# Shared scatter banks for the last two expert pairs, another order of value products, and three smaller edits, in an encoder layer

## The chip, the cores and the metric

The kernel runs on one core of a Trainium2 chip. The metric is the device time of one execution in microseconds (us). The core has a matmul engine (TensorE, PE in the profile; PEld is its weight load), a vector engine (VectorE, DVE), a scalar engine (ScalarE, ACT), GpSimd (POOL) and SyncE (SP), which here issues the DMA transfers. PE adds up products in PSUM, which has eight banks of 512 fp32 values per partition; the other engines read the sums from there.

## The reference

One layer of an encoder on 512 tokens of 1024 channels, with a final norm, all in fp32:

```python
h = rms_norm(x);  u = h @ w_in
c = silu(layer_norm(depthwise_conv31(glu(u[:, :512]))))      # 256 channels
a = dilated_attention(rotary(q), rotary(k), v)               # 12 heads of 64, 3 branches
x = x + concat(rms_norm(c), rms_norm(a)) @ w_out
x = x + cross_attention(rms_norm(x), rms_norm(mem))          # 4 heads of 256, 256 memory tokens
h = rms_norm(x)                                              # expert layer from here
group = top1(softmax(h @ w_group + b_group))                 # 4 groups
two experts = top2 of the group's 8 by h @ w_router + b_router
for each expert e: y_e = (silu(h @ w1[e]) * (h @ w3[e])) @ w2[e]   # 512 hidden columns
x = x + gate1 * y_e1 + gate2 * y_e2
out = rms_norm(x)
```

## The kernel before

**Tokens and precision.** The 512 tokens are four tiles of 128 (`NT = 4`). Where operands are rounded to the fp32r format, a value is split into a high part and the remainder, and the products run with both; `split` (line 109) lets ACT copy the high half and DVE (or the engine given as `eng`) subtract it from the value (line 115).

**Attention.** The 12 heads run in six pairs. `head_softmax` makes, for each of a head's four query tiles, the scores (lines 560 and 561), a masked maximum, the exponential (ACT, line 569) and the reciprocal of the sum, and GpSimd multiplies the row with it (line 572, tile `pw`). `head_transposed` turns each `pw` on PE (line 582) and collects the result in `pt`, two query tiles per `pt`. `attend_out` then makes the value products of a pair (line 596): two halves of the queries (256 columns each), four key tiles, two heads; head 0 writes partitions 0 to 63 of the PSUM tile `o` and head 1 partitions 64 to 127. This part is written in program order, and a list scheduler with priorities places the instructions of each engine: at each step the engine takes, of what is ready by its model, the piece of highest priority. GpSimd also has the convolution's taps (lines 423, 424, 434, 435) and the last step of the rotary embedding (lines 504 and 505). PE's rows of line 147 that stand between these are products of the input projection for the following pairs.

**Route.** `route_tile` computes for each token tile the group, the two experts and the gates on small DVE operations (lines 901 to 954), the matrix `M` of chosen experts (line 925), and from that, by a product on PE, the rank `RK` of each token within its expert. It also fills `hm`, the normalised tokens in high and low halves that the gather products read. For the last tile (t = 3) ACT writes the scaled row `hn` first, and the low halves are made by GpSimd.

**Experts.** Each expert has 64 slots. The 32 experts run in 16 pairs. `hot` builds a one-hot matrix from `RK`; `take` gathers by products `hm` x one-hot; `put` stores the result as `xT`. Weights stream through a ring of regions in SBUF (`ring`, 512 KB per DMA, SP line 1014), issued in order as regions come free. `experts_up` and `experts_down` compute the hidden and the output rows with fp32 products of 64 columns; the scatter adds an expert pair's rows back to the tokens by a product with a one-hot matrix (`ct`) in PSUM, and DVE adds the PSUM bank to the residual `xacc` (line 1231). This part is written in the order in which it runs.

**The end.** `experts_last` handles the last pair, n + 3. Its output columns come in three groups: out(0) has columns 0 to 511, out(1) 512 to 767 and out(2) 768 to 1023. `between` scatters the pair before it, n + 2, with banks of its own. Then the norm: ACT (line 1332) or DVE (line 1343) sums squares of each tile and column group into `fss`; `finish_out` adds them up for all four tiles, GpSimd raises them to the power -0.5, and ACT and DVE scale the tiles, each of which SP then writes out.

Of the kernel before, what the change touches and what calls it, by code (L numbers as in the profile page):

```python
# [8 lines left out]
F32 = mybir.dt.float32  # L9
# [3 lines left out]
AF = mybir.ActivationFunctionType  # L13
# [71 lines left out]
class K:  # L85
# [502 lines left out]
    def attend_out(self, j, pts, v):  # L588

        nc = self.nc  # L590
        o = self.ps("o")
        vo = (j % 2) * 128
        for half in range(2):
            for kt in range(NT):
                for i in range(2):
                    nc.tensor.matmul(o[i * 64:i * 64 + 64, half * 256:half * 256 + 256],
                                     v[kt][:, vo + i * 64:vo + i * 64 + 64], pts[i][half][:, kt, :],
                                     start=kt == 0, stop=kt == NT - 1)
        self.split(o, self.aT[0][:, 2 + j, :], self.aT[1][:, 2 + j, :], scale=self.VT[:, V_AO + j:V_AO + j + 1])
        return o  # L600
# [284 lines left out]
    def route_tile(self, t, p, ss, rs, lgs):  # L885
# [35 lines left out]
        key2, k2 = keys(em, m2, NE, "b")  # L921
        oh2 = row("oh2", NE)
        V.tensor_scalar(oh2, key2, k2, None, op0=ALU.is_equal)
        M = self.M[:, t, :]
        V.scalar_tensor_tensor(M, no1, 0.0, oh2, op0=ALU.is_lt, op1=ALU.add)
        with self.tc.high_priority(offset=-60 if t < NT - 1 else 0):

            h = self.xacc[:, t, :]
            for b in range(2):
                c = slice(b * 512, b * 512 + 512)  # L930
                parts = lambda v: v.rearrange("q (b m) -> q b m", b=2)
                hi, lo = parts(self.hm[t][:, 0, c]), parts(self.hm[t][:, 1, c])
                turned = h[:, c].rearrange("q (m b) -> q b m", b=2)
                if t < NT - 1:
                    self.split(turned, hi, lo, scale=r)
                else:
                    hn = self.rh.tile([128, 512], F32, name="hn", tag="hmT")
                    nc.scalar.activation(parts(hn[:]), turned, AF.Copy, scale=r)
                    self.split(hn, self.hm[t][:, 0, c], self.hm[t][:, 1, c], eng=nc.gpsimd)

            gx, gs = row("gx", NG), one("gs")
            ngm = one("ngm")
            V.tensor_scalar(ngm, gm, -1.0, None, op0=ALU.mult)
            nc.scalar.activation(gx, gl, AF.Exp, bias=ngm, scale=1.0, accum_out=gs)
            e2 = one("e2")
            V.tensor_tensor(e2, m2, m1, op=ALU.subtract)
            nc.scalar.activation(e2, e2, AF.Exp)
            g1 = one("g1")
            V.scalar_tensor_tensor(g1, e2, 1.0, gs, op0=ALU.add, op1=ALU.mult)
            V.reciprocal(g1, g1)  # L950
            V.tensor_tensor(e2, e2, g1, op=ALU.mult)
            G = self.G[:, t, :]
            V.tensor_scalar(G, no1, 0.0, g1, op0=ALU.is_lt, op1=ALU.mult)
            V.scalar_tensor_tensor(G, oh2, e2, G, op0=ALU.mult, op1=ALU.add)
# [78 lines left out]

    def hot(self, oh, d, t):

        self.nc.vector.tensor_tensor(oh[:, t, :].rearrange("p (e s) -> p e s", s=CAP),
                                     self.iota[:].unsqueeze(1).to_broadcast([128, 4, CAP]),
                                     self.RK[:, t, 4 * d:4 * d + 4].unsqueeze(2).to_broadcast([128, 4, CAP]), op=ALU.is_equal)

# [18 lines left out]
    def first_gather(self):  # L1058


        oh, xT = self.slots()
        ps = [self.ps(tag) for tag in ("tr", "s", "s", "tr")]

        def add(t, chunks=range(DC)):
            if chunks[0] == 0:
                self.hot(oh, 0, t)
            for cc in chunks:
                self.take(ps[cc // 2], oh, cc, t, t == 0 and cc % 2 == 0, t == NT - 1 and cc % 2 == 1)

        def end():  # L1070
            x = xT()
            put = lambda chunks: [self.put(x, ps[cc // 2], cc) for cc in chunks]

            def rest():
                add(NT - 1, range(DC // 2, DC))
                put(range(DC // 2, DC))

            put(range(DC // 2))
            return oh, x, rest
        return add, end  # L1080
# [152 lines left out]
    def experts(self, gathered):  # L1233
# [8 lines left out]
        with self.in_order():  # L1242
            gt = None
            for d in range(NE // 4 - 1):
# [21 lines left out]
                if d:  # L1266
# [16 lines left out]
            ys, ct = None, c2  # L1283
            self.hidden_turned((n + 3,))
            ys = self.experts_down(n + 2, now[:, 0:1])
        self.experts_last(n + 3, self.hidden(n + 3), ct[:, 1, :], now[:, 1:2],
                          lambda: self.scatter_pair(ct[:, 0, :], ys, end))

    def experts_last(self, pr, hT, ct, gt, between):

        self.finish_begin()
        y2 = [self.wsp.tile([128, 2, 512], F32R, name="y2", tag="whi") for _ in range(2)]
# [2 lines left out]
        def out(j, before=None):  # L1295
            c0, c1 = groups[j]
            w = ((lambda e, k: self.piece(pr, 2, k, None)[:, e, :]) if j == 0 else
                 (lambda e, k: self.last_piece(j - 1, k)[:, e, :]))
            ys = self.outputs(w, hT, gt, c1 - c0, y2[j % 2], before)
            return [(ct, ys)], c0, c1 - c0, ("o", "m", "tr", "tr")  # L1300

        with self.in_order():
            first = out(0)
            between()
            self.scatter(*first)
            todo = out(1)
        self.finish_part(0, 0, 512, range(NT))
        with self.queued():
            last = out(2, lambda: self.scatter_tile(0, *todo))
            for t in range(1, NT):  # L1310
                self.scatter_tile(t, *todo)
            self.finish_part(1, 512, 768, range(NT))
            self.scatter(*last, lambda t: self.finish_last(t))
            self.finish_out()

    def finish_begin(self):

# [18 lines left out]

    def finish_last(self, t):

        if t < NT // 2:
            self.finish_part(2, 768, D, [t])  # L1340
        else:
            x = self.xacc[:, t, 768:D]
            self.nc.vector.tensor_tensor_reduce(self.fk[:, 0:256], x, x, 1.0 / D, 0.0, ALU.mult, ALU.add,
                                                self.fss[:, t, 2:3])

    def finish_out(self):

        nc = self.nc
        r = self.frs
        nc.vector.tensor_reduce(r, self.fss[:], AX.X, ALU.add)  # L1350
        nc.vector.tensor_scalar(r, r, 1e-6, None, op0=ALU.add)
        nc.gpsimd.tensor_tensor(r, r, self.mhalf[:, 0:NT], op=ALU.pow)
        for t in range(NT):
            fo = self.fo[t]
            nc.scalar.activation(fo[:, 0:512], fo[:, 0:512], AF.Copy, scale=r[:, t:t + 1])
            nc.vector.scalar_tensor_tensor(fo[:, 512:D], self.xacc[:, t, 512:D], r[:, t:t + 1], self.fg[:, 512:D],  # L1356
                                           op0=ALU.mult, op1=ALU.mult)
            nc.sync.dma_start(self.a["out"][0, t * 128:t * 128 + 128, :], fo)

    def overflow(self, pool):  # L1360

# [259 lines left out]
```

## Time and profile before

| | |
|---|---|
| time, median of three runs | 949.62 us (948.07 to 950.01) |
| time of the profiled execution | 948.14 us |
| its span in the trace | 946.4 us |
| mean granted clock of PE | 0.99 |
| PE busy | 921.4 us, 97% |
| PEld / DVE / ACT / POOL busy | 642.7 / 480.2 / 302.7 / 203.7 us |
| DMA | 243.63 MB, mean 257 GB/s |

The profile is of one execution; all times within it count from the start of its span. Busy shares are means over stages that differ: the projections and the attention until about 210, out projection and cross-attention until 458, the route of the last tile until 464, the experts until 919, and the tail. A row of the timeline gives start, duration, engine, line, operation, and the tiles written and read; an `x` at the end counts the instructions that were joined in the row. A bracket gives how long the engine was idle before and which result ended that. Each value product of 64 columns is two instructions in the trace.

### The profile page before, as it was taken

How to read it: one execution, taken by the hardware profiler on the slowest of the kernel's cores; microseconds unless marked ns; L12 is line 12 of the kernel's file. 1: busy time of each engine (PE TensorE's matmuls, PEld its weight loads, DVE VectorE, ACT ScalarE, POOL GpSimd, SP SyncE). 2: the span in 40 equal slices, each digit the busy share in tenths (PEclk: the TensorE clock that was granted, in tenths of full speed). 3: DMA queues.
4: the chain of work that ended last, by engine and by line, in shares of the span. 5: the costliest groups of instructions: out<-in, count | busy, mean ns of one | idle time of the engine just before them, and what ended most of it. 6: DMA issues, size and time to landing. Idle time of an engine off the chain costs nothing. (4 is left out here: it accounts for less than half of the span.)

```text
span 946.4 us, 15348 instructions
## 1 busy us (share of the span) xinstructions
PE 921.4 (97%) x5788; PEld 642.7 (68%) x5788; DVE 480.2 (51%) x1136; ACT 302.7 (32%) x685; POOL 203.7 (22%) x245
## 2 busy tenths in 40 slices
PE   8998999999999999999899999999999999999994
PEld 7988889988899988999645453544535445354442
DVE  6569778688857544646512160432604325043345
ACT  6525467656633444535301110101101011010113
POOL 3249999993310001100100000000000000000002
PEclk9999999999999999999999999999999999999997
DMA  7431121132365123691699999999999999999992
GB/s 223 137 89 45 46 68 43 49 112 90 110 215 179 45 90 119 235 357 38 228 410 369 409 393 400 408 409 410 409 409 409 409 409 409 409 409 409 408 379 104
DMA packets 102889, 243.63 MB, mean 257 GB/s; under 512 B 11304, under 2 KB 51612, under 8 KB 102812
## 3 DMA queue, kind: packets, MB, share of 16 engines
q1 hardware_dynamic: 102812, 242.62, 67.9%
q8 instruction: 47, 0.77, 0.3%
q14 instruction: 30, 0.25, 0.1%
HBM read 240.49 MB, written 2.10 MB: 256 GB/s over the span
## 5 line engine op out<-in xcount | busy, mean ns | idle before, releaser
L147 PE MATMUL ps_pj<-ring,xT 128*64 128x512 f32 x504 | 111.8, 594 | 0.3 <-DVE xT L1052 0.3
L147 PE MATMUL ps_s<-ring,xT 128*64 128x512 f32 x488 | 106.1, 592 | 0.0
L1335 POOL TENSOR_TENSOR ring<-xacc,ring 128x512 f32<-128x512 f32 x4 | 5.0, 1280 | 466.9 <-DVE xacc L1231 466.9
L115 DVE TENSOR_TENSOR wlo<-wst,whi 128x512 fp32r<-128x512 f32 x104 | 82.5, 824 | 30.8 <-ACT whi L114 30.3
L147 PEld LDWEIGHTS ps_pj<-ring,xT 128*64 128x64 f32 x504 | 35.9, 137 | 70.1 <-issue 66.9
L147 PEld LDWEIGHTS ps_s<-ring,xT 128*64 128x64 f32 x488 | 35.1, 137 | 69.3 <-issue 64.8
L114 ACT ACTIVATE whi<-wst 128x512 fp32r<-128x512 f32 x108 | 62.5, 625 | 46.6 <-issue 12.7
L147 PE MATMUL ps_pj<-whi,hT_hi 128*128 128x256 f32 x256 | 74.3, 291 | 0.9 <-DVE rv L502 0.9
L147 PE MATMUL ps_pj<-wlo,hT_hi 128*128 128x256 f32 x256 | 74.4, 291 | 0.0
L147 PE MATMUL ps_pj<-whi,hT_lo 128*128 128x256 f32 x256 | 73.8, 289 | 0.0
L147 PE MATMUL ps_o<-ring,eT 128*64 128x512 f32 x238 | 62.1, 596 | 0.0
L147 PE MATMUL ps_m<-ring,eT 128*64 128x512 f32 x238 | 61.7, 592 | 0.0
L147 PEld LDWEIGHTS ps_pj<-onehot,hm 128*128 128x128 f32 x448 | 54.5, 191 | 10.3 <-issue 4.9
L147 PE MATMUL ps_pj<-onehot,hm 128*128 128x256 f32 x448 | 57.5, 286 | 0.3 <-ACT gt L1118 0.3
L1160 DVE TENSOR_TENSOR sl<-sl,ps_s 128x512 f32<-128x512 f32 x8 | 5.5, 688 | 102.4 <-PE ps_s L147 102.4
L1160 DVE TENSOR_TENSOR sl<-sl,ps_pj 128x512 f32<-128x512 f32 x8 | 5.5, 687 | 96.9 <-PE ps_pj L147 86.2
L1198 ACT ACTIVATE ys<-ps_o,gt 128x512 fp32r<-128x512 f32 x15 | 10.3, 687 | 130.9 <-PE ps_o L147 130.9
L147 PEld LDWEIGHTS ps_pj<-whi,hT_hi 128*128 128x128 f32 x256 | 49.4, 193 | 2.8 <-PE ps_tr L532 1.1
L147 PEld LDWEIGHTS ps_pj<-whi,hT_lo 128*128 128x128 f32 x256 | 49.6, 194 | 1.2 <-issue 0.8
L147 PEld LDWEIGHTS ps_pj<-wlo,hT_hi 128*128 128x128 f32 x256 | 49.5, 194 | 1.3 <-issue 0.4
L1201 DVE SCALAR_TENSOR_TENSOR ys<-ps_o,gt,ys 128x512 fp32r<-128x512 f32 x15 | 11.3, 751 | 75.7 <-ACT ys L1198 75.7
L569 ACT ACTIVATE pw<-pw,nm 128x512 f32<-128x512 f32 x48 | 34.5, 720 | 35.9 <-DVE nm L567 32.2
(391 smaller groups left out, 2068.9 us busy)
## 6 DMA issues: line engine op xcount, KB each, us to landing
ring<-in_w_dram SPq DMA_DIRECT2D x371, 512.0 KB
wst<-in_w_in_dram SPq DMA_DIRECT2D x24, 256.0 KB
wst<-in_w_in_dram SPq DMA_DIRECT2D x10, 512.0 KB
first<-in_w_dram SPq DMA_DIRECT2D x9, 512.0 KB
wst<-in_w_xk_dram SPq DMA_DIRECT2D x8, 512.0 KB
wst<-in_w_xv_dram SPq DMA_DIRECT2D x8, 512.0 KB
wst<-in_w_out_dram SPq DMA_DIRECT2D x8, 512.0 KB
wst<-in_w_xq_dram SPq DMA_DIRECT2D x8, 512.0 KB
```

What stands on the lines that cost most here:

```text
L114: nc.scalar.activation(hi, src, AF.Copy)
L115: (eng or nc.vector).tensor_tensor(lo, src, hi.bitcast(F32), op=ALU.subtract)
L147: ins = self.nc.tensor.matmul(*args, **kw)
L569: nc.scalar.activation(w, w, AF.Exp, bias=nm, scale=0.125, accum_out=den)
L1160: nc.vector.tensor_tensor(sl, sl, hs[1], op=ALU.mult)
L1198: nc.scalar.activation(ys[:, 0, 0:n], p[:, 0:n], AF.Copy, scale=gt)
L1201: nc.vector.scalar_tensor_tensor(ys[:, 1, 0:n], p[:, 0:n], gt, ys[:, 0, 0:n].bitcast(F32), op0=ALU.mult, op1=ALU.subtract)
L1335: nc.gpsimd.tensor_tensor(self.fo[t][:, 0:512], x, self.fg[:, 0:512], op=ALU.mult)
```

## The change

The change has four edits. In `attend_out` the loop over halves runs 1, 0 and the loop over heads 1, 0. In `route_tile` the low halves of the last tile are no longer made by GpSimd: they are kept in a list, and the first gather's `add` issues them on DVE behind `hot`. In `experts_last` the pairs n + 2 and n + 3 add into the same PSUM banks: `begun` opens four banks with pair n + 2's products for columns 0 to 511, `ended` adds pair n + 3's and closes them, and `both` does both pairs at once for the two other column groups. In `finish_out` norm scales are made for two tiles at a time, and the scaling of all four tiles stands behind the second two.

```diff
@@ -590,9 +590,10 @@
         nc = self.nc
         o = self.ps("o")
         vo = (j % 2) * 128
-        for half in range(2):
+
+        for half in (1, 0):
             for kt in range(NT):
-                for i in range(2):
+                for i in (1, 0):
                     nc.tensor.matmul(o[i * 64:i * 64 + 64, half * 256:half * 256 + 256],
                                      v[kt][:, vo + i * 64:vo + i * 64 + 64], pts[i][half][:, kt, :],
                                      start=kt == 0, stop=kt == NT - 1)
@@ -921,6 +922,7 @@
...
+        self.rest = rest = []
...
@@ -936,7 +938,8 @@
                 else:
                     hn = self.rh.tile([128, 512], F32, name="hn", tag="hmT")
                     nc.scalar.activation(parts(hn[:]), turned, AF.Copy, scale=r)
-                    self.split(hn, self.hm[t][:, 0, c], self.hm[t][:, 1, c], eng=nc.gpsimd)
+                    nc.scalar.activation(self.hm[t][:, 0, c], hn, AF.Copy)
+                    rest.append((self.hm[t][:, 1, c], hn, self.hm[t][:, 0, c].bitcast(F32)))
 
             gx, gs = row("gx", NG), one("gs")
             ngm = one("ngm")
@@ -1033,7 +1036,7 @@
 
     def hot(self, oh, d, t):
 
-        self.nc.vector.tensor_tensor(oh[:, t, :].rearrange("p (e s) -> p e s", s=CAP),
+        return self.nc.vector.tensor_tensor(oh[:, t, :].rearrange("p (e s) -> p e s", s=CAP),
                                      self.iota[:].unsqueeze(1).to_broadcast([128, 4, CAP]),
                                      self.RK[:, t, 4 * d:4 * d + 4].unsqueeze(2).to_broadcast([128, 4, CAP]), op=ALU.is_equal)
 
@@ -1063,7 +1066,10 @@
 
         def add(t, chunks=range(DC)):
             if chunks[0] == 0:
-                self.hot(oh, 0, t)
+                with self.behind(self.hot(oh, 0, t)):
+                    while t == NT - 1 and self.rest:
+                        lo, h, hi = self.rest.pop(0)
+                        self.nc.vector.tensor_tensor(lo, h, hi, op=ALU.subtract)
             for cc in chunks:
                 self.take(ps[cc // 2], oh, cc, t, t == 0 and cc % 2 == 0, t == NT - 1 and cc % 2 == 1)
 
@@ -1283,10 +1289,10 @@
             ys, ct = None, c2
             self.hidden_turned((n + 3,))
             ys = self.experts_down(n + 2, now[:, 0:1])
-        self.experts_last(n + 3, self.hidden(n + 3), ct[:, 1, :], now[:, 1:2],
-                          lambda: self.scatter_pair(ct[:, 0, :], ys, end))
-
-    def experts_last(self, pr, hT, ct, gt, between):
+        self.experts_last(n + 3, self.hidden(n + 3), ct, ys, now[:, 1:2])
+
+    def experts_last(self, pr, hT, ct, ys, gt):
+
 
         self.finish_begin()
         y2 = [self.wsp.tile([128, 2, 512], F32R, name="y2", tag="whi") for _ in range(2)]
@@ -1296,22 +1302,50 @@
             c0, c1 = groups[j]
             w = ((lambda e, k: self.piece(pr, 2, k, None)[:, e, :]) if j == 0 else
                  (lambda e, k: self.last_piece(j - 1, k)[:, e, :]))
-            ys = self.outputs(w, hT, gt, c1 - c0, y2[j % 2], before)
-            return [(ct, ys)], c0, c1 - c0, ("o", "m", "tr", "tr")
+            return self.outputs(w, hT, gt, c1 - c0, y2[j % 2], before)
+
+        def begun():
+
+            banks = []
+            for t in range(NT):
+                p = self.ps(("tr", "tr", "pj", "pj")[t])
+                for i in range(2):
+                    self.mm(p, ct[:, 0, t * 128:t * 128 + 128], ys[0][:, i, :], start=i == 0, stop=False)
+                banks.append(p)
+            return banks
+
+        def ended(y, t, p):
+
+            for i in range(2):
+                self.mm(p, ct[:, 1, t * 128:t * 128 + 128], y[:, i, :], start=False, stop=i == 1)
+            xs = self.xacc[:, t, 0:512]
+            self.nc.vector.tensor_tensor(xs, xs, p, op=ALU.add)
+
+        def both(j, y, t):
+
+            c0, c1 = groups[j]
+            self.scatter_tile(t, [(ct[:, 0, :], ys[1][:, :, c0 - 512:c1 - 512]), (ct[:, 1, :], y)], c0, c1 - c0,
+                              ("o", "m", "tr", "tr"))
 
         with self.in_order():
-            first = out(0)
-            between()
-            self.scatter(*first)
-            todo = out(1)
+            y = out(0)
+            banks = begun()
+            for t in range(NT):
+                ended(y, t, banks[t])
+            y = out(1)
         self.finish_part(0, 0, 512, range(NT))
         with self.queued():
-            last = out(2, lambda: self.scatter_tile(0, *todo))
-            for t in range(1, NT):
-                self.scatter_tile(t, *todo)
+            last = out(2)
+            for t in range(NT):
+                both(1, y, t)
             self.finish_part(1, 512, 768, range(NT))
-            self.scatter(*last, lambda t: self.finish_last(t))
-            self.finish_out()
+            for t in range(NT):
+                both(2, last, t)
+                if t % 2 == 0:
+                    self.finish_part(2, 768, D, [t])
+                else:
+                    self.finish_last(t)
+                    self.finish_out(t - 1)
 
     def finish_begin(self):
 
```

How the order moves, at three places. First PE, in the attention of the first pair: value products (line 596 before, 597 after; `o` is their PSUM bank), the end of the stretch where the second part of them stands before, and the same place after. `x8` counts products as written, two instructions each. Before:

```order
L582 MATMUL ps_tr<-early,pw 128x128 x4
L147 MATMUL ps_pj<-whi,hT_hi 128x256
L147 MATMUL ps_pj<-wlo,hT_hi 128x256
L147 MATMUL ps_pj<-whi,hT_lo 128x256
L596 MATMUL ps_o<-pt,v 64x256 x8
L560 MATMUL ps_s<-kh,qs 128x512
L561 MATMUL ps_s<-kl_515,qs 128x512
L147 MATMUL ps_pj<-whi,hT_hi 128x256
L147 MATMUL ps_pj<-wlo,hT_hi 128x256
L147 MATMUL ps_pj<-whi,hT_lo 128x256
```

and a little later, before:

```order
L147 MATMUL ps_pj<-whi,hT_lo 128x256
L147 MATMUL ps_pj<-whi,hT_hi 128x256
L596 MATMUL ps_o<-pt,v 64x256 x7
L582 MATMUL ps_tr<-early,pw 128x128 x8
L147 MATMUL ps_pj<-wlo,hT_hi 128x256
```

After:

```order
L147 MATMUL ps_pj<-wlo,hT_hi 128x256
L147 MATMUL ps_pj<-whi,hT_lo 128x256
L597 MATMUL ps_o<-pt,v 64x256 x16
L582 MATMUL ps_tr<-early,pw 128x128 x8
L147 MATMUL ps_pj<-whi,hT_hi 128x256
L147 MATMUL ps_pj<-wlo,hT_hi 128x256
```

Before, eight products stand in front of a pair of score products, seven in front of eight transposes, and one further back; after, all 16 stand in one place, in front of the eight transposes. In the same stretch GpSimd's order changes too; `pw` is a normalisation, `ctmp` and `sg` are convolution taps, `qr` is rotary. Before:

```order
L572 TENSOR_SCALAR pw<-pw,rd 128x512
L424 TENSOR_TENSOR sg<-sg,ctmp 128x512
L423 TENSOR_SCALAR ctmp<-cpad,vt 128x512
L572 TENSOR_SCALAR pw<-pw,rd 128x512
L424 TENSOR_TENSOR sg<-sg,ctmp 128x512
L504 TENSOR_TENSOR qr<-ru,rv 128x4x32
L505 TENSOR_TENSOR qr<-rv,ru 128x4x32
L572 TENSOR_SCALAR pw<-pw,rd 128x512
L423 TENSOR_SCALAR ctmp<-cpad,vt 128x512
L572 TENSOR_SCALAR pw<-pw,rd 128x512
```

After:

```order
L505 TENSOR_TENSOR qr<-rv,ru 128x4x32
L423 TENSOR_SCALAR ctmp<-cpad,vt 128x512
L504 TENSOR_TENSOR qr<-ru,rv 128x4x32
L505 TENSOR_TENSOR qr<-rv,ru 128x4x32
L424 TENSOR_TENSOR sg<-sg,ctmp 128x512
L423 TENSOR_SCALAR ctmp<-cpad,vt 128x512
L424 TENSOR_TENSOR sg<-sg,ctmp 128x512
L423 TENSOR_SCALAR ctmp<-cpad,vt 128x512
L424 TENSOR_TENSOR sg<-sg,ctmp 128x512
L504 TENSOR_TENSOR qr<-ru,rv 128x4x32
L505 TENSOR_TENSOR qr<-rv,ru 128x4x32
L572 TENSOR_SCALAR pw<-pw,rd 128x512
```

The ten rows of before hold the normalisations no. 15 to 18; in the twelve rows of after, two pieces of rotary and three taps stand ahead of no. 16.

Second DVE, at the route of the last tile: `RK` are the ranks, `onehot` is what `hot` writes, `rkT` the ranks turned, `xT` the first gathered tokens. Before:

```order
L962 SCALAR_TENSOR_TENSOR RK<-ps_o,M 128x32
L954 SCALAR_TENSOR_TENSOR G<-oh_6024,e_6040,G 128x32
L1036 TENSOR_TENSOR onehot<-iota,RK 128x256
L115 TENSOR_TENSOR ghl<-G,ghl 128x8x4
L973 TENSOR_REDUCE cm<-ps_o 128x1
L1100 CAST rkT<-ps_m 32x512
L975 CAST cnt<-cm 128x1
L1052 TENSOR_SCALAR xT<-ps_tr,gmo 128x256 x2
L1052 TENSOR_SCALAR xT<-ps_s,gmo 128x256 x2
```

After:

```order
L965 SCALAR_TENSOR_TENSOR RK<-ps_o,M 128x32
L957 SCALAR_TENSOR_TENSOR G<-oh_6024,e_6038,G 128x32
L1039 TENSOR_TENSOR onehot<-iota,RK 128x256
L1072 TENSOR_TENSOR hm<-hn,hm 128x512 x2
L115 TENSOR_TENSOR ghl<-G,ghl 128x8x4
L976 TENSOR_REDUCE cm<-ps_o 128x1
L1106 CAST rkT<-ps_m 32x512
L1055 TENSOR_SCALAR xT<-ps_tr,gmo 128x256 x2
L978 CAST cnt<-cm 128x1
L1055 TENSOR_SCALAR xT<-ps_s,gmo 128x256 x2
```

The two subtractions that write `hm` stand behind the one-hot tile and ahead of the rank cast.

Third DVE, at the end: `y_` are output rows of the last pair, `ISA` at line 1343 (1374 after) is the sum of squares. Before:

```order
L1231 TENSOR_TENSOR xacc<-xacc,ps_tr 128x256 x2
L1231 TENSOR_TENSOR xacc<-xacc,ps_o 128x256
L1231 TENSOR_TENSOR xacc<-xacc,ps_m 128x256
L1231 TENSOR_TENSOR xacc<-xacc,ps_tr 128x256
L1343 ISA ring,fss<-xacc 128x256
L1343 ISA fss 128x1
L1231 TENSOR_TENSOR xacc<-xacc,ps_tr 128x256
L1343 ISA ring,fss<-xacc 128x256
L1343 ISA fss 128x1
L1350 TENSOR_REDUCE frs<-fss 128x4
L1351 TENSOR_SCALAR frs<-frs 128x4
L1356 SCALAR_TENSOR_TENSOR ring<-xacc,frs,ring 128x512 x4
```

After:

```order
L1237 TENSOR_TENSOR xacc<-xacc,ps_o 128x256
L1237 TENSOR_TENSOR xacc<-xacc,ps_m 128x256
L1374 ISA ring,fss<-xacc 128x256
L1374 ISA fss 128x1
L1380 TENSOR_REDUCE frs<-fss 128x2
L1381 TENSOR_SCALAR frs<-frs 128x2
L1237 TENSOR_TENSOR xacc<-xacc,ps_tr 128x256 x2
L1374 ISA ring,fss<-xacc 128x256
L1374 ISA fss 128x1
L1380 TENSOR_REDUCE frs<-fss 128x2
L1381 TENSOR_SCALAR frs<-frs 128x2
L1387 SCALAR_TENSOR_TENSOR ring<-xacc,frs,ring 128x512 x4
```

The reduction and the scale of two tiles stand ahead of the last two tiles' adds, and the second two tiles have their own.

## Rows read from the trace of the kernel before

**Rows 1.** Windows: stretch, us, busy us of engines (instructions), PE clock, DMA share, GB/s.

```profile
core 0: us, PE busy (x) PEld busy (x) DVE busy (x) ACT busy (x) POOL busy (x), PEclk, DMA share, GB/s
71.00:118.00 47.00, 42.55 (x318) 38.16 (x317) 40.74 (x83) 22.01 (x45) 46.12 (x49) 0.96 0.16 46
118.00:458.00 340.00, 339.55 (x2583) 313.13 (x2582) 227.70 (x626) 181.55 (x421) 124.79 (x155) 1.00 0.38 129
464.00:919.00 455.00, 454.67 (x2358) 219.21 (x2358) 144.85 (x273) 52.86 (x119) 0.00 (x0) 1.00 1.02 402
```

**Rows 2.** Timeline of PE at value products and scores (start us, us, engine, line, operation).

```profile
119.10 0.65 PE L596 MATMUL ps_o<-pt,v 128*64 128x256 f32 x2
...
135.30 1.95 PE L596 MATMUL ps_o<-pt,v 128*64 128x256 f32 x16
137.18 0.50 PE L560 MATMUL ps_s<-kh,qs 128*128 128x512 f32 x1
137.51 0.39 PE L561 MATMUL ps_s<-kl,qs 128*128 128x512 f32 x1
138.98 1.94 PE L596 MATMUL ps_o<-pt,v 128*64 128x256 f32 x14
```

**Rows 3.** Groups of POOL, 71 to 213: instructions, busy us, mean ns, idle before.

```profile
L424 POOL TENSOR_TENSOR sg<-sg,ctmp 128x512 f32<-128x512 f32 x27 | 38.7, 1432 | 1.1
L572 POOL TENSOR_SCALAR pw<-pw,rd 128x512 f32<-128x512 f32 x36 | 28.5, 794 | 0.8 <-DVE rd L571 0.8
L423 POOL TENSOR_SCALAR ctmp<-cpad,vt 128x512 f32<-128x512 f32 x27 | 23.0, 850 | 0.8
...
L505 POOL TENSOR_TENSOR qr<-rv,ru 128x128 f32<-128x128 f32 x19 | 12.0, 631 | 0.0
L504 POOL TENSOR_TENSOR qr<-ru,rv 128x128 f32<-128x128 f32 x19 | 10.2, 535 | 0.0
```

**Rows 4.** Timeline of PE at its longest wait for GpSimd.

```profile
110.06 0.66 PE L582 MATMUL ps_tr<-early,pw 128*128 128x128 f32 x4 [1.39 <-POOL pw L572]
```

**Rows 5.** Timeline at the route, an earlier tile's operation first, then the last tile.

```profile
442.57 0.24 DVE L919 TENSOR_SCALAR no<-akey,ak 128x32 f32<-128x32 f32 x1
...
457.53 2.51 POOL L115 TENSOR_TENSOR hm<-hn,hm 128x512 fp32r<-128x512 f32 x2 [2.05 <-ACT hm L114]
...
457.58 1.28 DVE L919 TENSOR_SCALAR no<-akey,ak 128x32 f32<-128x32 f32 x1
...
458.89 1.20 DVE L907 CUSTOM_DVE_ANT_0 em<-em,no 128x32 f32<-128x32 f32 x1
...
460.07 2.23 SPq L1014 DMA_DIRECT2D ring<-in_w_dram  x2
...
461.16 0.18 PE L147 MATMUL ps_o<-M,ltb 128*128 128x32 bf16 x1 [2.28 <-DVE M L925]
```

**Rows 6.** Group of DVE's subtractions of 128x512 from SBUF, 262 to 460.

```profile
L115 DVE TENSOR_TENSOR wlo<-wst,whi 128x512 fp32r<-128x512 f32 x36 | 23.3, 687 | 16.1 <-ACT whi L114 15.8
```

**Rows 7.** Timeline of the tail.

```profile
919.86 1.20 PE L147 MATMUL ps_pj<-ys,ct 128*128 128x512 f32 x4
...
924.51 0.70 PE L147 MATMUL ps_o<-y,ct 128*128 128x512 f32 x2 [0.74 <-DVE xacc L1231]
...
926.60 3.67 PE L147 MATMUL ps_s<-ring,eT 128*64 128x256 f32 x32
...
933.93 0.42 DVE L1231 TENSOR_TENSOR xacc<-xacc,ps_tr 128x256 f32<-128x256 f32 x1
...
935.37 1.01 POOL L1352 TENSOR_TENSOR frs<-frs,mhalf 128x4 f32<-128x4 f32 x1 [3.37 <-DVE frs L1351]
...
937.23 2.95 SPq L1358 DMA_DIRECT2D out_dram<-ring  x4
```

**Rows 8.** Windows in the expert stage and the tail, and SP's waits from 500 to 520.

```profile
504.00:516.00 12.00, 12.00 (x57) 4.08 (x58) 0.83 (x3) 0.84 (x2) 0.00 (x0) 1.00 0.94 329
920.00:925.00 5.00, 4.26 (x18) 3.08 (x18) 4.37 (x8) 0.67 (x1) 0.00 (x0) 1.00 0.62 222
...
SPq L1014 <- PE ps_pj L147: 9.7, 5, 5.7
```

More of the change, by code (lines that the diff above doesn't have):

```diff
@@ L1337, in finish_last, with finish_out @@
     def finish_last(self, t):
[L1339 to L1346, printed above, removed]
+        x = self.xacc[:, t, 768:D]
+        self.nc.vector.tensor_tensor_reduce(self.fk[:, 0:256], x, x, 1.0 / D, 0.0, ALU.mult, ALU.add, self.fss[:, t, 2:3])
+    def finish_out(self, t0):
         nc = self.nc
-        r = self.frs
-        nc.vector.tensor_reduce(r, self.fss[:], AX.X, ALU.add)
+        r = self.frs[:, t0:t0 + 2]
+        nc.vector.tensor_reduce(r, self.fss[:, t0:t0 + 2, :], AX.X, ALU.add)
         nc.vector.tensor_scalar(r, r, 1e-6, None, op0=ALU.add)
[L1352 to L1358, printed above, removed]
+        nc.gpsimd.tensor_tensor(r, r, self.mhalf[:, 0:2], op=ALU.pow)
+        if t0:
+            for t in range(NT):
+                fo = self.fo[t]
+                nc.scalar.activation(fo[:, 0:512], fo[:, 0:512], AF.Copy, scale=self.frs[:, t:t + 1])
+                nc.vector.scalar_tensor_tensor(fo[:, 512:D], self.xacc[:, t, 512:D], self.frs[:, t:t + 1],
+                                               self.fg[:, 512:D], op0=ALU.mult, op1=ALU.mult)
+                nc.sync.dma_start(self.a["out"][0, t * 128:t * 128 + 128, :], fo)
     def overflow(self, pool):
```

## The prediction

> **What bounds the kernel now.** I read the page's busy shares first and then the stage windows [rows 1]. The reader should see that TensorE (PE) leaves nothing over in the two long stages: 339.55 of 340 us from 118 to 458 (rest of attention, out projection, cross-attention) and 454.67 of 455 us from 464 to 919 (experts). Time is left in three places only: 71 to 118, where PE is busy 42.55 of 47 us at a granted clock of 0.96 while GpSimd (POOL) is busy 46.12; the route of the last token tile around 460; and the tail behind 920. So in the dense stages a change is worth the PE time that it takes out, provided POOL still delivers in time, and in the two gaps it is worth what it takes off the chain of the waiting engine. The change touches all of these.
>
> **Value products (edit of `attend_out`).** Timeline of PE, line 596 [rows 2]: a product as written is two instructions, so eight products (x16) in one stretch take 1.95 us, seven (x14) take 1.94 and one (x2) takes 0.65. Seven cost what eight do: two neighbours, one of each head and each on 64 columns of the array, run side by side, and an odd one at the end of a stretch has no partner. Before, a pair's 16 products come as 8, 7 and 1: 1.87 + 1.87 + 0.58 = 4.32 by the step to the next instruction, which is some 0.07 below the duration. That is 0.15 for a stretch and 0.43 for each two products begun. After, the order shows all 16 in one stretch: 8 × 0.43 + 0.15 = 3.59. Over the six pairs, with two irregular ones (4, 4, 7, 1 and 6, 2, 7, 1 before; 6 + 10 once after) I add up 26.2 before and 21.7 after: −4.5. A score product right behind such a stretch takes 0.50 where the next takes 0.39 [rows 2]; some nine such seams go, −0.9. Together −5.3 of PE work, at 71 to 207.
>
> What can take it back is POOL, which works almost without a pause there (46.12 of 47 us in the first third). The scheduler, which sees other ready times, gives POOL another order: two more convolution taps and two more rotary pairs stand ahead of the 18th normalisation (line 572). By the row means [rows 3] before has 18 × 0.794 + 18 × (1.432 + 0.850) + 10 × (0.535 + 0.631) = 67.0 us to the end of no. 18; after has 18 × 0.794 + 20 × 2.282 + 12 × 1.166 + 0.6 (a small power operation that now stands there, an estimate) = 74.5, so +7.5. The same sum for no. 17, 25 and 28 gives +6.1, +8.0 and +4.3; at no. 31 it is −0.8, at no. 36 +1.9. The transposes that need these normalisations also move back in PE's order: PE's work ahead of them grows by 3.4, 5.0, 4.4 and 4.8. What is not covered (about 2.7, 2.5, 3.6 and nothing) partly overlaps with slack, since before there are only two such waits, the longer 1.39 [rows 4]. Carried through in order I get new PE waits of 1.6, 0.3, 1.2 and 1.6 in place of the old, and POOL's last normalisation about 1.8 late: the stage keeps −3.5 of the −5.3. Bounds: −5.4 if all is covered, 0 if POOL sets the stage's end; the value is the sum by order.
>
> **Low halves of the last tile on the vector engine (DVE).** In the route of tile 3 POOL subtracts twice, 457.53 to 460.04. In the same 2.5 us two small DVE operations take 1.28 and 1.20 us, which for an earlier tile take 0.24 [rows 5] and, by the same timeline, 0.19: 2.05 us lost on the chain that ends with M at 461.1, for which PE waits 2.28. After, POOL does nothing there, so M, ranks and the one-hot tile (`hot`) come up to 2.05 earlier. But behind `hot` DVE now has two subtractions of 128x512 at 0.687 [rows 6], 1.37 in all, ahead of the rank cast and the token put; PE's products with the low halves wait for them. Net −0.7 (bounds 0, if the stretching had another cause and PE's queue covers the lows, to −2.05). The first two ring loads are issued at 460.07, when POOL's subtraction frees them [rows 5]; after, they wait for DVE's second subtraction, at about 461.5 in the same frame, 1.4 later.
>
> **Tail (shared banks, norm scales by two tiles).** Before [rows 7]: out(0) is done at 919.86, eight tile scatters of pair n+2 and four of n+3 follow, and out(1) and out(2) come only at 926.60, 3.67 us for both; the last add is 933.93 to 934.35, square, sum and scale lead to POOL's power at 935.37 (1.01), then scaling, and the first output is issued at 937.23. After: `begun` 8 products in steps of 0.26 (four take 1.20 there, of which the last part lies beside the next four) from 919.86 to 921.9; `ended` 8 more to 923.7 (less by what the two share); out(1) 1.8 to 925.4, out(2) to 927.2; `both` for two column groups, 32 products of 256 columns at half of that, some 0.135, to 931.5. PE has no bank wait left in between, for the adds that held it (0.74 at 924.51) are eight fewer; they lie on DVE beside PE and count only by that wait. The last add then ends about 932.6 (DVE's lag behind PE at the end, about 1 us, is kept), the second reduce and scale 933.6. Tiles 0 and 1 have their power already and are scaled first, so the first output goes out at 934.5 in place of 937.23: −2.7. From there the four outputs take as long as before. Bounds: −1.0, if only the power's 1.01 goes, and −3.5, if DVE follows PE at once. A later pair 2 half costs nothing as long as its weights have landed; out(2) needs the last ones at about 924.5, and the stream had moved all before 925 (222 GB/s in 920 to 925 against 402 in the stage [rows 1, 8]).
>
> **Sum.** −3.5 − 0.7 − 2.7 = −6.9 on the profiled execution's 948.14 (span 946.4): 941.2. The median of the runs, 949.62, is 1.48 above the profiled one; I add it: 942.7. The expert stage itself is not shortened.
>
> **Rivals.** First, the weight stream sets the time of the expert stage and PE's earlier start there is partly lost. For it: DMA share 1.02 at 402 GB/s, and the later first loads. Against it: in 504 to 516 the stream runs at only 329 GB/s with SP waiting 9.7 us for PE to free regions of the ring [rows 8]; so the stream is ahead of PE and is gated anew by PE, and moves forward with it. If the 1.4 us of the later loads is not made up: 942.7 + 1.4 = 944.1. The Trainium skill ("Trainium Kernel Development and Optimization", the opening note on reading a trace) calls busy matmul time a bad metric and the busy share of weight loads a good one. By that rule the expert stage, whose weight loads are busy 219.21 of 455 us [rows 1], is not PE-bound, which is this rival; the 329 GB/s row speaks against it.
>
> Second, POOL is what paces attention, and the PE time removed turns into waits: nothing in 71 to 213, 949.62 − 3.4 = 946.2. For it: POOL's 46.12 of 47 us and the sums above; against it: the dense 339.55 of 340 from 118 on, where POOL is never waited for.
>
> Third, the new order removes the two waits behind 108 us, and with them the lower clock: 0.96 as the mean of 47 us is a stretch of some 3.7 us at 1.2 in place of 2.4 GHz, which costs half of that, some 1.8: 942.7 − 1.8 = 940.9.
>
> Fourth, slower: POOL's later normalisations hold PE. If the 25th arrives the whole 8.0 us later and PE's own moves cover none of it, PE loses 8.0 there, gains the 1.8 that is saved behind it, pays 3.6 for two more half-clock stretches of the third rival's price, and 3.4 comes back in route and tail: 949.62 + 8.0 − 1.8 + 3.6 − 3.4 = 956.0. It decides against the change once PE's waits for POOL from 118 to 207, nearly nothing now, sum above about 8.6. Against it: the transposes stand later in PE's order as well. The Trainium skill ("TensorE: Matmul & The Clock Gate", on how clock oscillation bites in real kernels) has bursts of products between waits pay the lower clock each time anew; one such stretch is in the trace, behind the waits of [rows 4], and the rule would make more waits cost more than their length.
>
> **How the numbers follow.** Forecast as summed 0.60 (its own range 940.5 to 945.5), stream 0.11, no gain in attention 0.12, clock regained 0.10, slower 0.07. No change is within 0.2% of the median, 947.7 to 951.5, about what a measurement of this kernel tells; a third of the second rival's spread falls in it, and a little of the fourth's. So faster 0.86, same 0.08, slower 0.06. The range goes from below the third rival, with the tail at its better bound, 938.8, to above the second, 947.2; what is left out is the fourth and the far side of each.
>
> **What would show it.** Value products of line 597 in rows of 32 with a step near 3.6 and PE from 71 to the route some 3.5 shorter, with a few PE waits on `pw` of 0.3 to 1.6 in 118 to 207. Line 919's and 907's operations (lines 920 and 908 after) at 0.24 and 0.19 in tile 3, the wait on M nearly gone, and a wait of PE for DVE's `hm` instead. Out(2) on PE by 927 less the shift, the first output 2.7 earlier against out(0). It would be wrong if POOL waits of PE sum to more than 5, if SP or DMA waits appear on PE in the expert stage, or if out(1) waits for its weights.

## The result and the profile after

The changed kernel takes 944.77 us (median of 5 runs, 943.96 to 945.92), the kernel before in the same session 949.73: ratio 0.9949, 95% interval 0.9938 to 0.996, so 4.8 us faster (3.8 to 5.9). Forecast were 942.7 in a range of 938.8 to 947.2. The profiled execution took 944.69 us with a span of 942.9.

Windows of the kernel after, columns as in [rows 1]:

```profile
71.00:118.00 47.00, 42.88 (x335) 39.01 (x334) 43.20 (x90) 23.31 (x48) 46.20 (x49) 1.00 0.17 47
118.00:160.00 42.00, 38.53 (x294) 34.79 (x293) 28.73 (x78) 25.07 (x51) 40.91 (x51) 0.96 0.17 50
160.00:213.00 53.00, 51.83 (x415) 47.03 (x414) 41.15 (x103) 34.87 (x75) 51.38 (x58) 1.00 0.25 81
213.00:458.00 245.00, 243.69 (x1862) 229.39 (x1861) 152.96 (x442) 120.00 (x293) 34.57 (x48) 1.00 0.45 152
```

and of the kernel before, for the two middle stretches:

```profile
118.00:160.00 42.00, 42.00 (x318) 37.46 (x317) 34.40 (x89) 30.15 (x61) 41.27 (x52) 1.00 0.17 51
160.00:213.00 53.00, 53.00 (x407) 46.17 (x406) 41.15 (x101) 31.57 (x70) 50.69 (x57) 1.00 0.25 81
```

PE, which was never idle from 118 to 213, now is for 3.47 + 1.17 us, and the lower clock that stood in 71 to 118 stands in 118 to 160. POOL is as busy as before. What PE waited for in 71 to 215 (engine, line, releaser: us in total, times, longest), before:

```profile
PE ps_tr L582 <- POOL pw L572: 2.1, 2, 1.4
PE ps_tr L532 <- POOL qr L505: 1.5, 1, 1.5
PE ps_pj L147 <- DVE rv L502: 0.9, 1, 0.9
```

and after:

```profile
PE ps_tr L582 <- POOL pw L572: 4.9, 5, 3.2
PE ps_tr L532 <- POOL qr L505: 1.2, 1, 1.2
PE ps_m L447 <- POOL sg L435: 1.0, 1, 1.0
PE ps_pj L147 <- DVE rv L502: 0.9, 1, 0.9
PE ps_tr L532 <- DVE pt L108: 0.5, 1, 0.5
PE ps_tr L582 <- DVE kl L541: 0.3, 1, 0.3
```

The waits grow by 4.3 us, most of it one wait, which ends at 143.40. The timeline of PE there, and then that of POOL:

```profile
143.40 0.47 PE L582 MATMUL ps_tr<-early,pw 128*128 128x128 f32 x1 [3.20 <-POOL pw L572]
143.80 5.15 PE L597 MATMUL ps_o<-pt,v 128*64 128x256 f32 x32
```

```profile
139.81 0.69 POOL L423 TENSOR_SCALAR ctmp<-cpad,vt 128x512 f32<-128x512 f32 x1
140.59 1.26 POOL L424 TENSOR_TENSOR sg<-sg,ctmp 128x512 f32<-128x512 f32 x1
141.81 0.45 POOL L504 TENSOR_TENSOR qr<-ru,rv 128x128 f32<-128x128 f32 x1
142.22 0.45 POOL L505 TENSOR_TENSOR qr<-rv,ru 128x128 f32<-128x128 f32 x1
142.65 0.69 POOL L572 TENSOR_SCALAR pw<-pw,rd 128x512 f32<-128x512 f32 x1
```

POOL is working on a tap and a rotary pair while PE waits for the normalisation behind them. PE falls idle at 140.20, and the reciprocal that the normalisation needs (DVE, line 571) is made at 141.23 or 141.46; so at most 1.3 of the 3.2 us lie with POOL's order at this place; the rest is the time up to the reciprocal and the normalisation itself. One transpose (x1) of the normalised tile stands ahead of the pair's value products, and the other three stand behind them, at 148.88. The products therefore cannot need its result; they wait only because it is in front of them.

They then run at half clock: the granted clock is 0.50 from 143.4 to 145, 1.2 in place of 2.4 GHz, behind the idle 3.2 us, and the row takes 5.15 us, where it takes 3.67 at full clock in an experiment below. In the balance of the two traces the clock cancels, since the stretch that before has in 71 to 118 (0.96 of 47 us, some 1.9) is gone. The weights of the first score product were loaded at 59.92 in the trace before and at 60.65 here; the last tile's line 919 (now 920) stood at 457.58 and stands at 457.84. Windows from the one to the other, before and after:

```profile
59.92:457.58 397.66, 392.76 (x2977) 361.46 (x2976) 278.90 (x730) 206.64 (x473) 180.20 (x212) 1.00 0.35 118
60.65:457.84 397.19, 387.13 (x2977) 360.12 (x2976) 276.04 (x730) 206.60 (x473) 182.06 (x211) 1.00 0.35 118
```

PE is busy for 5.6 us less and idle for 5.2 us more (10.06 in place of 4.90). Attention and everything up to the route gained 0.5 us in these two traces.

The route after, to be held against [rows 5]:

```profile
457.84 0.24 DVE L920 TENSOR_SCALAR no<-akey,ak 128x32 f32<-128x32 f32 x1
458.12 0.19 DVE L908 CUSTOM_DVE_ANT_0 em<-em,no 128x32 f32<-128x32 f32 x1
459.38 0.18 PE L147 MATMUL ps_o<-M,ltb 128*128 128x32 bf16 x1 [0.25 <-DVE M L927]
460.29 1.28 DVE L1072 TENSOR_TENSOR hm<-hn,hm 128x512 fp32r<-128x512 f32 x2
461.74 3.37 SPq L1017 DMA_DIRECT2D ring<-in_w_dram  x3
462.81 2.37 PE L147 MATMUL ps_pj<-ring,xT 128*64 128x512 f32 x10 [0.69 <-DVE xT L1055]
```

The two DVE operations are short again, the wait for M is 0.25 in place of 2.28, the two subtractions stand behind the one-hot tile, and the first ring load is issued 1.67 us later than before. The experts start at 462.81, 1.02 earlier than before in the trace (463.83), having been 0.26 late at line 919: 1.28 gained. From there to out(0)'s end PE needs 456.45 us, before 456.03: 0.4 is lost again in this trace, 0.17 of it in a wait for weights at 918.25.

The tail after, to be held against [rows 7]:

```profile
919.26 1.20 PE L147 MATMUL ps_tr<-ys,ct 128*128 128x512 f32 x4
923.13 3.72 PE L147 MATMUL ps_s<-ring,eT 128*64 128x256 f32 x32
931.46 0.70 POOL L1382 TENSOR_TENSOR frs<-frs,mhalf 128x2 f32<-128x2 f32 x1 [1.64 <-DVE frs L1381]
932.88 2.76 DVE L1387 SCALAR_TENSOR_TENSOR ring<-xacc,frs,ring 128x512 f32<-128x512 f32 x4
933.05 1.14 POOL L1382 TENSOR_TENSOR frs<-frs,mhalf 128x2 f32<-128x2 f32 x1 [0.88 <-DVE frs L1381]
933.70 2.91 SPq L1389 DMA_DIRECT2D out_dram<-ring  x4
```

From out(0)'s end to the first output it is 14.44 us, before 17.37: 2.93 gained. Scaling starts before the second power is done. The parts make up the difference of the two spans, 946.4 and 942.9: 0.5 up to the route, 1.3 in it, −0.4 in the expert stage and 2.9 in the tail, less the 0.7 by which the first score product came later.

### The profile page after: what moved, and what is told of

It reads as the page before. It is cut to its first block, busy times and chain, and to the rows that moved or that the text cites. A ratio compares the mean times of both kernels' runs of the same rounds, so it can differ in the third digit from the quotient of the medians.

```text
span 942.9 us, 15352 instructions
## 1 busy us (share of the span) xinstructions
PE 915.8 (97%) x5796; PEld 642.4 (68%) x5796; DVE 472.2 (50%) x1132; ACT 302.8 (32%) x685; POOL 203.9 (22%) x244
## 4 chain that ended last, share of the span: by engine, by line
PE 78%; DVE 7%; POOL 6%; DMA 3%; issue 2%; ACT 1%; SPq 1%; DVEq 0%; ACTq 0%; POOLq 0%
PE ps_pj L147 34%; PE ps_s L147 20%; PE ps_o L147 7%; PE ps_m L147 7%; PE ps_tr L147 2%; DVE wlo L115 2%; POOL sg L435 2%; PE ps_tr L151 1%; PE ps_o L597 1%; DVE pw L565 1%; POOL pw L572 1%; POOL sg L424 1%; DMA ring<-in_w_dram 1%; DVE sg L430 1%; DMA wst<-in_w_in_dram 1%
```

## The experiments

Each was timed in five rounds beside the kernel before; ratios are to that, with 95% intervals, and differences in us follow the ratios where medians are not named. The change has two smaller edits, the low halves and the scales, and not three as the title says. First the four edits one by one.

**e1_value_order.** The loops of `attend_out` alone (`for half in (1, 0)`, `for i in (1, 0)`).

> Value products in the new order only; everything else as before. Theory 1 (GpSimd takes it back): PE's work from 71 to 458 falls by about 4, but waits for GpSimd's normalisations grow from 2.1 to about 5 us and one of some 3.2 near 143 brings a half-clock stretch; net -0.5 to -2.0 against before. Theory 2 (the forecast: the waits stay near those of before and most of the PE work is gained): -3.5. Theory 3 (slower through the waits): +2 or more.

Measured: 949.6, ratio 0.9995 (0.9986 to 1.0004). Its PE waits in 71 to 213 are those of the changed kernel, 4.9 on normalisations with 3.2 at 143. Theory 1, at its low end, −0.5 by the ratio, which cannot be told from no change; the forecast's −3.5 is outside the interval.

**e2_lows_vector.** The low halves alone (`rest`, and in `add` the subtractions on DVE behind `hot`).

> Only the last tile's low halves moved to DVE behind the one-hot tile. Theory 1 (GpSimd's subtraction stretches DVE's small operations beside it): line 919's and 907's operations fall from 1.28 and 1.20 to 0.24 and 0.19, PE's wait for M from 2.28 to below 0.5, the expert stage starts 1.0 to 1.3 earlier and the time falls by 0.7 to 1.3. Theory 2 (the weight stream sets the expert stage): same start gain, but the first ring loads are later and the end does not move: 0.0.

Measured: 947.55, ratio 0.9982 (0.9973 to 0.9991), −1.7 us: theory 1, with more gain than its start shows in the trace. In its trace the experts start 0.94 earlier than before (462.89), out(0) ends 0.47 earlier (919.39), and PE meets one wait for weights near the end:

```profile
918.38 1.08 PE L147 MATMUL ps_s<-ring,eT 128*64 128x512 f32 x4 [0.27 <-DMA ring<-in_w_dram]
```

So in this trace about half of the start's gain stays, 0.5. The edit is not shown to cost the other half: e8, with the same late loads, needs 456.03 us from the experts' start to out(0)'s end, as before does, and e1, whose low halves are on GpSimd, needs 456.52, with a wait for weights of 0.2. Another part of the 1.7 may be in executions that the profile of before isn't one of. In the traces of the kernels whose low halves are on GpSimd, the mean clock in 452 to 476 is 1.00 for three (before, e3, e6) and 0.93 for four (e1, e4, e9, e10); it is 1.00 in all seven whose low halves are on DVE (after, e2, e5, e7, e8, e11, e12). A window of the scale experiment e4, 2.7 us behind PE's wait for M, which ends at 461.31 there:

```profile
464.00:466.00 2.00, 2.00 (x7) 0.80 (x8) 0.63 (x2) 0.84 (x2) 0.00 (x0) 0.54 0.57 223
```

0.93 over 24 us is 1.7 us. At four times in seven that would be 1.0 on average; with the start's gain of 0.5, or of 1.3 where nothing is lost behind it, the sum lies in the measured 0.9 to 2.6. The share is an estimate from one trace per kernel, and how the 1.7 splits is not shown.

**e3_banks.** Shared banks alone (`begun`, `ended`, `both`), scales for four tiles at the end as before.

> Only the last two pairs' shared banks; norm scales still for four tiles at once. Theory 1 (eight fewer adds and no bank wait): from out(0)'s end to the last add 12.8 in place of 14.5 us, time -1.7. Theory 2 (the gain of the tail is nearly all the power's, not the banks'): -0.5 or less.

Measured: 947.06, ratio 0.9976 (0.9966 to 0.9986), −2.3 us. Theory 1. From out(0)'s end to the first output it takes 15.27 us (920.66 to 935.93) against 17.37.

**e4_scales.** Scales by two tiles alone: in the last scatter, `finish_part` for even tiles, `finish_last` and `finish_out(t - 1)` for odd ones.

> Only norm scales by two tiles, scatters as before. Theory 1 (the power operation leaves the path to the first output, the rest of the chain stays): first output about 1.2 earlier against out(0)'s end, time -1.2. Theory 2 (one output later than the first sets the end, so only part is gained): -0.5.

Measured: 949.32, ratio 1.0 (0.9991 to 1.0009): neither theory's gain; the distance from out(0) to the first output is 16.97, and to the end of the span 26.3 against 26.5. The timeline says why:

```profile
934.96 0.42 ACT L1332 ACTIVATE ring<-xacc 128x256 f32<-128x256 f32 x1
935.28 0.19 ACT L1332 ACTIVATION_READ_ACCUMULATOR ring<-xacc 128x1 f32 x1
935.50 0.16 DVE L1346 TENSOR_REDUCE frs<-fss 128x2 f32<-128x6 f32 x1 [0.47 <-ACT ring L1332]
935.69 0.17 DVE L1347 TENSOR_SCALAR frs<-frs 128x2 f32<-128x2 f32 x1
935.77 0.74 DVE L1231 TENSOR_TENSOR xacc<-xacc,ps_tr 128x256 f32<-128x256 f32 x2
```

The first sum over tiles 0 and 1 waits for ACT's square of tile 0's last columns (934.96), which stands on ACT behind the squares of the earlier column group, and the last adds stand behind the sum on DVE. With shared banks out(1) and its squares come earlier, the same wait is 0.17, and the scales are worth the difference of 15.27 and 14.44, 0.8. In the traces the two edits of the tail are worth a little more together (2.93) than apart (2.10 and 0.40).

The four add up to −0.5 − 1.7 − 2.3 + 0.0 = −4.5. To see what holds attention, work was then taken off GpSimd.

**e5_after_act_norm and e6_before_act_norm.** After, and before, each with one edit:

```diff
-            nc.gpsimd.tensor_scalar(w, w, rd, 1.0, op0=ALU.mult, op1=ALU.mult)
+            if t == NT - 1:
+                nc.scalar.activation(w, w, AF.Copy, scale=rd)
+            else:
+                nc.gpsimd.tensor_scalar(w, w, rd, 1.0, op0=ALU.mult, op1=ALU.mult)
```

> The changed kernel, and besides the normalisation of each head's last query tile (12 of 48) done by ACT, which takes 12 x 0.794 = 9.5 us off GpSimd. Theory 1 (GpSimd sets the pace of attention, so the PE work saved by the value products could not show): PE's waits for GpSimd (4.9 + 1.2 + 1.0 us in 71 to 213) and the half-clock stretch behind the 3.2 us one mostly go, and the time falls by 4 to 6 against the changed kernel's 944.8, to 939 to 941. Theory 2 (GpSimd does not pace it; PE or the scheduler's order does): within 1 of the changed kernel.

> The kernel before, with the same 12 normalisations on ACT. Theory 1: with GpSimd out of the way PE, with its 5.3 us of dearer value products, is the next bound; the waits of 2.1 + 1.5 us and some of the half-clock stretch go: -2 to -4 against before, and the distance between this and the changed kernel with the same edit is about 9, 4 more than between changed and before. Theory 2: no change against before, distance 5 as between changed and before.

Measured: 945.26, ratio 0.9962 (0.9949 to 0.9975), and 949.47, 0.9998 (0.9988 to 1.0007). Nothing gained in either: theory 1 in the form "so many us less on GpSimd, so many less in all" falls. The waits remained: PE waits 2.84 for a normalisation at 144.19 in e5, with 5.2 us on normalisations in all, and rotary steps are waited for longer (2.6 and 2.5 us). In the order of both, GpSimd has taps and rotary steps ahead of normalisations as it had without the edit. But the edit does more than take work off GpSimd: the scheduler gives PE another order from 77 us on in both, so these two kernels don't settle whether GpSimd's load is what matters.

**e7_after_act_norm_24 and e11_act_norm_24_no_value_order.** The same edit with `t % 2 == 1` (24 of 48), on the changed kernel and on the changed kernel without its value order.

> The changed kernel with 24 of 48 normalisations on ACT (query tiles 1 and 3): 19 us off GpSimd, 15 us more on ACT. Theory 1: no more waits for GpSimd; PE is the bound then, so at most 1 to 2 us below the kernel with 12 of them on ACT. Theory 3 (ACT becomes the pace): 1 to 3 us above it. Theory 2: as the changed kernel.

> The three other edits without the value product order, and 24 of 48 normalisations on ACT. If the value order gives something only when GpSimd has less to do, this is 2 or more slower than the changed kernel with 24 on ACT (944.1); if the order gives nothing in any of these, it is within 1 of it.

Measured: 944.08 (943.0 to 945.31), ratio 0.994 (0.9927 to 0.9952), and 946.66 (945.84 to 947.56), 0.9968 (0.9956 to 0.998). e7 is not distinguishable from the changed kernel; but with 19 us less on GpSimd the value order is worth 2.6 us, where it was worth 0.5 in e1. This is weak support, for e11 is no faster than the same kernel without the normalisations on ACT (e8 below, 0.9955): from the first score product to the route its trace takes 1.4 us longer than e8's, and e7's takes 1.4 less than the changed kernel's. In both PE now has a wait of some 2.5 for DVE's line 567 (at 90.43 and 88.46), which neither had before, and e7's wait of 3.2 for a normalisation, at 145.09, is still there.

**e8_no_value_order.** The three other edits.

> The changed kernel without its value product order (the three other edits only). Theory 1: the value products give nothing, so the same as the changed kernel, -4.6 to -5.0 against before. Theory 2 (the order gives something once the route is shorter): -3.5 or less against before.

Measured: 945.13, ratio 0.9955 (0.9942 to 0.9969): theory 1, within the interval of the changed kernel.

**e9_fewer_taps and e10_fewer_taps_value_order.** Before, and e1, each with the loop over the taps of the first 128 channels cut from 31 to 11 (`range(KW - 20)`). Neither computes the layer; they leave out 20 taps.

> The kernel before with 20 of the 31 convolution taps of the first 128 channels left out, which takes 20 x (0.85 + 1.43) = 45.6 us of work off GpSimd, and so out of the engine's order among the normalisations. It is the base for the next kernel. Theory A (GpSimd's taps, standing in its order ahead of normalisations and rotary steps, and slowing DVE beside them, are what holds attention): PE's waits of 2.1 + 1.5 + 0.9 us and the half-clock stretch behind them go, -3 to -6 against before. Theory B (attention is held by the chain of scores, maximum, exponential and transposes, whatever GpSimd does besides): within 1.5 of before.

> The same 20 taps left out, with the new value product order (nothing else of the change). Theory A: with GpSimd out of the way PE's saved work of about 4 to 5 us shows, so 3.5 to 5 below the previous kernel. Theory B: the saving is lost in the chain here too, within 1.5 of the previous kernel, and PE's idle time in 71 to 213 is larger by about what its busy time is smaller.

Measured: 945.35 (944.48 to 947.25), ratio 0.9954 (0.9938 to 0.9971), and 941.81 (940.79 to 943.65), 0.9921 (0.9903 to 0.9938). Theory A: by the medians −3.9 without the taps, and now the value order brings 3.5 more, with ranges that don't touch; by the ratios −4.4 and 3.1, where theory A had 3.5 to 5. PE's group of the value products (busy us, mean ns of one) in e9:

```profile
L596 PE MATMUL ps_o<-pt,v 128*64 128x256 f32 x192 | 27.4, 388 | 0.0
```

and in e10:

```profile
L597 PE MATMUL ps_o<-pt,v 128*64 128x256 f32 x192 | 22.3, 383 | 0.0
```

The timeline of e9 at the start of the experts:

```profile
460.14 0.29 PEld L147 LDWEIGHTS ps_pj<-ring,xT 128*64 128x64 f32 x4 [0.23 <-DVE xT L1052]
```

and of e10, with a pair's 16 products before it as one row:

```profile
137.44 3.67 PE L597 MATMUL ps_o<-pt,v 128*64 128x256 f32 x32
...
456.10 0.20 PEld L147 LDWEIGHTS ps_pj<-ring,xT 128*64 128x64 f32 x4 [0.22 <-DVE xT L1053]
```

5.1 us less work on PE, and 4.0 of them arrive at the experts' start (both began at 59.7 with their scores). From the first score product to the route it is 4.9 (393.92 and 389.07), with PE idle for 3.4 and 4.4 us. The saving is real, and with the taps left out it shows. Here the other work hardly moves: apart from the taps, GpSimd's order is that of before in e9 until 208, and PE's until 154 in the time of before. Between e1 and e10 PE's order is the same up to the wait at 143; there e10 has the transpose behind the value products, which run without a wait at 137.44.

**e12_after_six_taps_dve.** A kernel that computes the whole layer, by the same reasoning: six more taps of the second 128 channels on DVE, which does a tap in one instruction.

```diff
-KDVE = 19
+KDVE = 25
```

> The changed kernel with six more convolution taps of the second 128 channels on DVE in place of GpSimd: 6 x (0.75 + 1.35) = 12.6 us off GpSimd, 6 x 1.0 us more on DVE; the result is the same layer. If GpSimd's work is what holds attention, the waits for its last tap (1.0) and some of those for normalisations go: 1 to 3 below the changed kernel's 944.8. If the one wait of 3.2 near 143, ahead of which nothing changes, is what matters, within 1 of it; if DVE's extra work delays the maxima, above it.

Measured: 943.38 (942.68 to 943.61), ratio 0.9928 (0.9912 to 0.9944): by the medians 5.9 faster than before, by the ratio 6.8, and its range lies below the changed kernel's (943.96 to 945.92), though the intervals of the two ratios overlap by a little. The wait for the last tap is gone and PE is busy throughout 160 to 213 (53.00 of 53); the wait of 3.1 is still there and ends at 145.25. All waits for normalisations are 5.9 in place of 4.9, and PE waits 1.0 for a maximum on DVE. From the first score product to the route the trace takes 396.70 us against the changed kernel's 397.19, with PE idle as long (10.0): the run is a little faster, but its trace does not show that less work on GpSimd shortened PE's waits.

## Why the prediction came out as it did

The sign and the range were right; the time forecast was 2 us too low, and the step that failed is one: **"the stage keeps −3.5 of the −5.3"**. Of it 0.5 shows in the two traces, and −0.5 in e1, which cannot be told from nothing. The work was sized well: −4.5 forecast for the products, 27.4 to 22.3 measured in e9 and e10, and for −5.3 in all (its two parts add up to −5.4) PE's busy time up to the route falls by 5.8 in the same two traces. GpSimd's later normalisations were seen too. Mis-sized was what they do: the sum had four waits of 0.3 to 1.6 in place of the old ones, and the trace has 5.2 us more of idle time, most of it one wait of 3.2 at 143. With the row means of POOL I had counted POOL's work alone, and PE's order by how much work stands ahead. The normalisation at 142.65 had its reciprocal from DVE (line 571) at 141.23 or 141.46 at the earliest, and then had the end of a tap and a rotary pair ahead of it; and a single transpose of it holds 16 value products. The half-clock stretch behind the wait (1.7) had no term either, but the one of 71 to 118 went, as in the third rival, so the two cancel. Two of the prediction's own signs of being wrong came: PE's waits for POOL sum to 7.1 in 71 to 215, over 5, and there is a wait for DMA in the expert stage, 0.17.

What happened in attention was the second rival, no gain there. I argued against it with a PE that was busy 339.55 of 340 us from 118 on. That was a weak argument: in e2 and e4, which have attention as before, but met no lower clock in 71 to 118 (1.00), PE was idle for 1.9 and 1.1 us in 118 to 213, and the route's line 919 began no earlier for it (457.92 and 457.73, before 457.58). A PE that is busy behind a half-clock stretch may only be catching up with an engine that it would otherwise wait for. That the total still came near the forecast is in part luck: the low halves brought 1.0 more than their term, and so made up for a third of the 3.0 that were missing here.

**Low halves:** forecast −0.7, measured −1.7 (−0.9 to −2.6). The rows came near what was foretold (0.24 and 0.19, M, `hot`, 1.28 for the two subtractions, ring loads at 461.7). The term was mis-sized: of the 2.04 by which M comes earlier against line 919, 0.76 is lost again behind M and not 1.37, so the experts start 1.28 earlier, and the same in e2 and e8. Not in the sum was a lower clock in the route, which the profile of before happened not to have, and which shows in no trace with the low halves on DVE. The first rival is not shown: the 0.4 that the expert stage takes longer here and in e2 is missing in e8. Adding 1.48 to the profiled execution as a constant took it for a loss that stays; how much of it is such a clock, which the edit takes away, is not shown.

**Tail:** forecast −2.7, 2.93 in the traces, so right as a sum. As a split it was not: I credited the power with at least 1.0, and alone the scales gave nothing.

The slower rival did occur in its first half: a wait with a half-clock stretch behind it. It was 3.2 + 1.7, and not that rival's 8.0 + 3.6.

What remains open is how the taps hold attention: by their place in POOL's order, by slowing DVE beside them (below), or by the order that the scheduler makes with them. An order with the taps kept and the one transpose behind the value products was not run; it would tell.

## What to carry to other kernels

Where a second engine works without pause next to a PE that does the same, price an edit that takes work from PE by taking work from the other engine first, in an experiment or in the sum; here the saving shows only there (with the taps 0.5 us, which cannot be told from nothing; 3.1 to 3.5 without). Take the work out rather than move it: with normalisations moved to ACT the order changed and PE met new waits of some 2.5. An edit that shortens a chain at its end may be worth nothing until another has made its inputs early. Before a profiled execution is taken as the frame of a sum, look where its clock fell, and whether the runs' median has another such place.

## What the runs showed of the hardware

DVE's subtractions of 128x512 (`wlo`, fp32 with an fp32r result) take much longer while GpSimd is working. The same group in 160 to 213, where POOL is busy 50.69 of 53 us in the kernel before, and 18.80 in e9. Before:

```profile
L115 DVE TENSOR_TENSOR wlo<-wst,whi 128x512 fp32r<-128x512 f32 x11 | 12.6, 1160 | 5.2 <-ACT whi L114 5.2
```

e9:

```profile
L115 DVE TENSOR_TENSOR wlo<-wst,whi 128x512 fp32r<-128x512 f32 x12 | 8.3, 714 | 4.9 <-ACT whi L114 4.9
```

1.16 us against 0.71, and 0.687 where POOL is busy 17.01 of 198 us [rows 6]. The maximum of the scores (line 565), which reads one of its two inputs from PSUM, has 0.68 in both. The Trainium skill ("SBUF — State Buffer", "SBUF: two separate sides") says that VectorE and GpSimd have one pair of SBUF ports between them, that the operation that starts first holds it for its whole length, and that a VectorE operation with two SBUF inputs is one that needs it; the rows agree in both directions, 1.16 for two SBUF inputs and 0.68 for one. In the route operations of 0.2 us took 1.28 and 1.20 beside POOL's subtraction [rows 5]. Line 907's has two SBUF inputs; line 919's has one and a scalar for each partition, so the sentence on two inputs does not cover it; that it is short without POOL's subtraction is shown (e2), by what it was held is not. I had not asked what such delays do in attention, where the two engines work beside each other for 140 us.
